# A two-layer decoder trunk on one core: tile addresses, the last down projection by token rows, and the first loads rearranged

## The chip, the core and the metric

The kernel runs on one core of one Trainium2 chip. The core has TensorE (matrix products, in the profile PE, with its weight loads as PEld), VectorE (DVE), ScalarE (ACT), GpSimd (POOL) and SyncE (SP, which here only issues DMAs). Operands lie in SBUF, 128 partitions wide; products are accumulated in PSUM, in 8 banks of 512 float32 columns. The metric is the device time of one execution in microseconds (us), as the median of several runs. One execution was also profiled.

## The reference

For one sequence of 256 tokens and width 1024, two layers of

```python
x = x + 0.5 * swiglu(rmsnorm(x, ffn1_norm[l]), ffn1_w_gate[l], ffn1_w_up[l], ffn1_w_down[l])
h = rmsnorm(x, mix_norm[l])
proj = h @ w_in[l]          # q, k/v, gates, GLA q/k/v, low rank, r, merge gates
o_a = nsa_attention(...)    # compressed, selected and window branches, 8 heads
o_b = gla_attention(...)    # gated linear attention, 4 heads, times silu(r)
y = gm[:, :, 0] * (o_a @ w_branch_nsa[l]) + gm[:, :, 1] * (o_b @ w_branch_gla[l])
x = x + y @ w_out[l]
x = x + 0.5 * swiglu(rmsnorm(x, ffn2_norm[l]), ffn2_w_gate[l], ffn2_w_up[l], ffn2_w_down[l])
```

and then `rmsnorm(x, final_norm)`. All is float32. `swiglu` is `(silu(x @ w_gate) * (x @ w_up)) @ w_down` with an inner width of 2816.

## The kernel before, in words

**Layout.** x is kept transposed: eight tiles of 128 features x 256 tokens. A product in float32 precision is made of three products of fp32r parts: an operand is split into a high part (a cast) and a low part (the rest). `mm3` (L122 to L124) issues high x high, high x low and low x high. `mm2` (L129, L130) does the same with two: the stationary weights' high part against a moving tile that holds high and low side by side (512 columns), then the weights' low part against the moving high part (256 columns). Each matmul loads its stationary tile of 128 columns again.

**Weights.** The class `Weights` streams 224 chunks of up to 128 x 2048 floats from HBM in the order of use. SP loads a chunk into one of three `raw` buffers, ACT casts the high part wh (L76), DVE subtracts to get the low part wl (L86), each in two halves; `prep` casts one half and subtracts the half before, and the program calls it twice a chunk, so that about one and a half chunks are ready ahead. Three pairs of wh and wl buffers take turns.

**Stages of a layer.** `ffn` (gate and up: 22 chunks of 16 rows, mm2 with x as the moving tile, profile name ff), down (16 chunks of 11 rows, name dn: eight output blocks of 22 products, mm2 for seven of them, mm3 for the last, with the hidden tiles h as moving tiles), `mixer` (T_pair products, name mm<-xs,wh, mm3 with 256 moving columns of x; the two vg chunks; 16 wr chunks, name mm<-wh,xs, in which a 128-token piece of x is stationary and 512 columns of weights move, mm3, in eight blocks of two chunks: v, v, r, r and four blocks of the merge gate gm; the merge, 6 wb chunks, name mg, the same form with oa and ob stationary; the output projection wo, 4 chunks, mm2 with y moving for seven of eight blocks), and `ffn` again. Attention and GLA run as generators whose steps are put between the mixer's matmuls (`slot`).

**Norms.** A norm's sum of squares goes through TensorE (`stat`, name st), then DVE (ms, L192) and a power on POOL (`rstd_col`, L194); `rstd_row` (name rb) turns it into a row with a product against the identity. The first chunk or two of a stage run before the norm is known; their results wait in PSUM (`wait`) and are scaled later.

**PSUM.** Two pools: `mm` with two banks and `sd` with six. The mixer's blocks take both banks of `mm`; a block of r leaves its banks by ACT (tanh) and then DVE (L541, which writes rt).

**Start.** ACT issues four loads of x and one of sm (all norm weights and biases); SP issues four loads of the first weight chunk, then the second chunk in three pieces and the third. Seven warm-up products (wb) run before the data come. Then x and chunk 0 are split in four steps, chunk 1 is cast, x is squared (L1153), the squares are summed on DVE (L1182 to L1185), and chunk 1's second half and chunk 2 are prepared.

**End.** In the last down projection the finished x blocks are multiplied by the final norm's weights and transposed back by TensorE (fin). After the last block come square, column sums (stl), power, four scalings, and four output DMAs on SP's queue.

**Addresses.** SBUF pools lie one behind the other in the order in which `go` opens them, each slot rounded to 32 bytes: const, small, sq, rb, t4 (15 tiles of 4096 bytes a partition, among them h, y, oa and ob), t2, raw, w. In the program before, the tiles of xs start at 128 modulo 512 bytes, and those of t4, t2, raw and of both w tags at 480 modulo 512. Weight rows of 128 columns, of 512 columns, and the high and low halves of a tile, lie at multiples of 512 bytes within their tiles.

## Time and profile before

| | |
|---|---|
| median of three runs | 1268.01 us (1267.92 to 1268.65) |
| profiled execution, whole | 1268.17 us |
| its span, first to last instruction | 1266.4 us |
| mean granted TensorE clock | 0.998 of full speed |
| busy share: PE, PEld, DVE, ACT, POOL | 99%, 85%, 72%, 56%, 4% |
| moved by DMA | 227.43 MB, 180 GB/s on average |

A row of a timeline gives the start, the length and the engine of an instruction, its source line, what it writes and reads, and in brackets how long its engine had been idle and what it waited for. The lengths of matmuls are modelled and overlap: what a matmul costs in a stream is the distance to the next start.

### The profile page before, as it was taken

The numbers are of one execution on the slowest core, as the hardware profiler recorded it, in microseconds if no ns is written. First come the engines' busy times: TensorE is split into PE (matmuls) and PEld (weight loads), VectorE is DVE, ScalarE is ACT, GpSimd is POOL, SyncE is SP. The second block draws the span as 40 slices with busy tenths as digits, with TensorE's granted clock in tenths as the row PEclk, the third lists the DMA queues.
The fourth block names the chain that finished last, engine by engine and source line by source line (L and its number), as shares of the span: only waits on it lengthen the run. The fifth ranks groups of instructions, "written<-read, shape, count | busy, mean of one in ns | idle before, by whom it ended". The sixth has DMA issues, their size and how long they took to land.

```text
span 1266.4 us, 18985 instructions
## 1 busy us (share of the span) xinstructions
PE 1251.6 (99%) x7396; PEld 1076.0 (85%) x7396; DVE 913.9 (72%) x1690; ACT 711.8 (56%) x1265; POOL 50.5 (4%) x60
## 2 busy tenths in 40 slices
PE   9999999999999999999999999999999999999997
PEld 7888889987778888888888888999777788888886
DVE  6888766774755778886578886567656668888753
ACT  5666545566644556655456664456675445566542
POOL 2001101000010000000010000010000100000000
PEclk9999999999999999999999999999999999999999
DMA  7576767334534445545665546573344354555451
GB/s 272 193 230 211 255 201 264 132 124 137 178 118 144 181 168 205 187 154 198 209 224 208 179 150 205 173 283 135 111 156 164 103 199 148 184 200 185 165 190 59
DMA packets 41001, 227.43 MB, mean 180 GB/s; under 512 B 6949, under 2 KB 8109, under 8 KB 21328
## 3 DMA queue, kind: packets, MB, share of 16 engines
q1 hardware_dynamic: 34352, 213.27, 48.7%
q0 software_dynamic: 5840, 11.87, 2.8%
q8 instruction: 58, 0.95, 0.3%
q10 hardware_dynamic: 720, 1.09, 0.3%
q14 instruction: 31, 0.25, 0.1%
HBM read 225.12 MB, written 2.63 MB: 180 GB/s over the span
## 4 chain that ended last, share of the span: by engine, by line
PE 80%; issue 15%; DVE 2%; ACT 2%; DMA 1%; POOL 0%; POOLq 0%; DVEq 0%; ACTq 0%
PE ff L129 19%; PE ff L130 10%; PE dn L129 9%; PE mm L122 7%; PE mm L123 6%; PE mm L124 6%; PE dn L130 4%; PE wo L129 2%; PE mg L122 2%; PE mg L124 2%; PE mg L123 2%; PE O L150 2%; PE o L150 1%; PE s L150 1%; PE wo L130 1%
## 5 line engine op out<-in xcount | busy, mean ns | idle before, releaser
L76 ACT ACTIVATE wh<-raw 128x1024 fp32r<-128x1024 f32 (+3 forms) x445 | 423.4, 967 | 183.6 <-issue 112.3
L86 DVE TENSOR_TENSOR wl<-raw,wh 128x1024 fp32r<-128x1024 f32 (+3 forms) x445 | 491.3, 1119 | 44.0 <-ACT wh L76 43.7
L129 PE MATMUL ff<-xs,wh 128*128 128x512 f32 x1408 | 489.9, 392 | 0.4 <-DVE xs L162 0.4
L130 PE MATMUL ff<-xs,wl 128*128 128x256 f32 x1408 | 393.9, 280 | 0.7 <-DVE wl L1144 0.5
L129 PEld LDWEIGHTS ff<-xs,wh 128*128 128x128 f32 x1408 | 264.4, 188 | 59.2 <-ACT wh L1143 0.8
L130 PEld LDWEIGHTS ff<-xs,wl 128*128 128x128 f32 x1408 | 264.3, 188 | 1.7 <-DVE wl L1144 1.1
L129 PE MATMUL dn<-h,wh 128*128 128x512 f32 x616 | 218.3, 399 | 0.0
L130 PE MATMUL dn<-h,wl 128*128 128x256 f32 x616 | 173.0, 281 | 0.0
L129 PEld LDWEIGHTS dn<-h,wh 128*128 128x128 f32 x616 | 115.7, 188 | 28.3
L139 DVE TENSOR_TENSOR u<-ff,u 128x256 f32<-128x256 f32 x176 | 74.7, 425 | 60.9 <-ACT u L138 60.9
L130 PEld LDWEIGHTS dn<-h,wl 128*128 128x128 f32 x616 | 116.4, 189 | 0.0
L122 PE MATMUL mm<-wh,xs 128*128 128x512 f32 x256 | 106.2, 415 | 2.5 <-DVE rt L541 2.5
L123 PE MATMUL mm<-wl,xs 128*128 128x512 f32 x256 | 101.5, 396 | 0.0
L124 PE MATMUL mm<-wh,xs 128*128 128x512 f32 x256 | 100.9, 394 | 0.0
L249 ACT ACTIVATE u<-u 128x256 f32<-128x256 f32 x88 | 36.8, 419 | 90.8 <-DVE u L248 90.8
L261 ACT ACTIVATE h<-u 128x256 fp32r<-128x256 f32 x88 | 36.8, 418 | 83.9 <-DVE u L260 83.9
L122 PE MATMUL mm<-xs,wh 128*128 128x256 f32 x256 | 73.8, 288 | 0.0
L124 PE MATMUL mm<-xs,wl 128*128 128x256 f32 x256 | 71.7, 280 | 0.0
L123 PE MATMUL mm<-xs,wh 128*128 128x256 f32 x256 | 71.6, 280 | 0.0
L138 ACT ACTIVATE u<-ff 128x256 f32<-128x256 f32 x176 | 65.6, 373 | 9.8 <-PE ff L130 5.4
L355 DVE SCALAR_TENSOR_TENSOR xs<-dn,xs 128x256 f32<-128x256 f32 x60 | 25.5, 424 | 56.0 <-PE dn L130 38.5
L122 PEld LDWEIGHTS mm<-wh,xs 128*128 128x128 f32 x256 | 48.1, 188 | 19.3 <-issue 4.7
(244 smaller groups left out, 1618.1 us busy)
## 6 DMA issues: line engine op xcount, KB each, us to landing
raw<-in_gu SPq DMA_DIRECT2D x85, 1024.0 KB, 4.9
raw<-in_wd SPq DMA_DIRECT2D x64, 704.0 KB, 4.1
raw<-in_wr SPq DMA_DIRECT2D x32, 1024.0 KB, 4.8
raw<-in_wt SPq DMA_DIRECT2D x16, 1024.0 KB, 5.1
raw<-in_wb SPq DMA_DIRECT2D x12, 1024.0 KB, 4.8
w<-in_w POOLq DMA_DIRECT2D x16, 512.0 KB, 8.6
raw<-in_wo SPq DMA_DIRECT2D x8, 1024.0 KB, 4.9
raw<-in_vg SPq DMA_DIRECT2D x4, 592.0 KB, 3.7
```

The source lines that it names most:

```text
L76: self.nc.scalar.activation(wh[:, s], self.raw[c][:, s], AF.Copy)
L86: self.nc.vector.tensor_sub(wl[:, s], self.raw[c][:, s], wh[:, s].bitcast(F32))
L122: mm(out, lh, rh, start=first, stop=False, skip_group_check=True)
L123: mm(out, lh, rl, start=False, stop=False, skip_group_check=True)
L124: mm(out, ll, rh, start=False, stop=last, skip_group_check=True)
L129: mm(b, lh, x[2], start=first, stop=False, skip_group_check=True)
L130: mm(b[:, 0:T], ll, x[0], start=False, stop=last, skip_group_check=True)
L138: self.nc.scalar.activation(o, b[:, T : 2 * T], AF.Copy)
L139: self.nc.vector.tensor_add(o, b[:, 0:T], o)
L150: self.nc.tensor.matmul(out, l, r, start=first, stop=last, skip_group_check=True)
L249: nc.scalar.activation(g, g, AF.Silu)
L261: nc.scalar.activation(hs[i][0], h, AF.Copy)
```

## The change

- The w tiles are 2176 instead of 2048 floats wide, and chunks whose weights move in 512 (or 296) columns (vg, wr, wb and the new wl) are written 40 floats further on. A tile of 128 floats that nothing uses is put ahead of t4, one of 88 floats ahead of w; the scratch of software DMAs is halved to 8192 bytes.
- The last down projection is computed with token rows in the partitions: 11 chunks of 4 rows of 512 columns, mm3 with h stationary; x comes in by products with the identity; squares, weights and scaling follow for each half of the features and of the tokens. The factor 0.5 goes into the gate of that stage. The final norm's weights come as a broadcast row from POOL's queue in chunk 11 of the gate and up stage.
- x's second to fourth loads are issued by SP, sm is the first load of ACT.
- The first norm's statistics come after chunk 1 instead of halfway through it, and its use in chunk 2; the first chunks' subtraction of wl comes ahead of the squares.
- The second block of r takes banks of `sd`.

```diff
+SHIFT = 40
...
-                self.pools["w"].tile([P, 2048], F32R, name=f"w{x}{c}", tag=f"w{x}") for x in "hl"
+                self.pools["w"].tile([P, 2176], F32R, name=f"w{x}{c}", tag=f"w{x}") for x in "hl"
...
-        self.nc.scalar.activation(wh[:, s], self.raw[c][:, s], AF.Copy)
+        self.nc.scalar.activation(wh[:, s.start + off : s.stop + off], self.raw[c][:, s], AF.Copy)
...
         def gate2(u):
-            nc.vector.tensor_mul(u[:, 0:T], u[:, 0:T], self.rbc)
+
+            if next_gain is None:
+                nc.vector.scalar_tensor_tensor(u[:, 0:T], u[:, 0:T], 0.5, self.rbc, op0=OP.mult, op1=OP.mult)
+            else:
+                nc.vector.tensor_mul(u[:, 0:T], u[:, 0:T], self.rbc)
...
+            late = i < 2 and start
+            if i == 1 + start:
+                self.rstd_row("mm" if start else "sd")
+                for n, b in enumerate(wait):
+                    u = gate(n, b[0])
+                    if start and n == 0:
+                        W.prep()
+                    gate2(u)
+                    up(n, u, b[1])
+            if not late:
                 u = gate(i, bs[0])
             W.prep()
...
+            if late:
+                self.stat("mm")
+                self.rstd_col()
+                self.constants()
+                wait.append(bs)
             else:
                 up(i, u, bs[1])
-                W.prep()
-            low()
+            W.prep()
+            if late:
+                continue
+            while len(lows) > 1:
+                low()
...
+        if next_gain is None:
+            self.last_down(hs)
+            return
...
+    def last_down(self, hs):
+
+        nc, W = self.nc, self.W
+        bs = [[self.bank(f"dn{e}{tt}", "sd" if e else "mm") for tt in range(2)] for e in range(2)]
+        pre = [self.small([P, 2], f"pre{tt}", 1) for tt in range(2)]
+        xg = [[self.t2(f"xg{e}{tt}") for tt in range(2)] for e in range(2)]
+
+        def residual(e):
+            for tt in range(2):
+                for q in range(4):
+                    self.mm(bs[e][tt][:, q * P : q * P + P], self.x[4 * e + q][:, tt * P : tt * P + P], self.ident, q == 0, False)
+
+        def products(c, tt, wh, wl):
+            for r in range(4):
+                e, k = divmod(4 * c + r, NFF)
+                s = slice(tt * P, tt * P + P)
+                self.mm3(bs[e][tt], hs[k][0][:, s], hs[k][1][:, s], wh[:, r], wl[:, r], False, k == NFF - 1)
+
+        def gained(e, tt):
+            sq = self.t2(f"fsq{e}{tt}")
+            nc.scalar.activation(sq, bs[e][tt], AF.Square, accum_out=pre[tt][:, e : e + 1])
+            nc.vector.tensor_mul(xg[e][tt], bs[e][tt], self.fin[:, e * 512 : e * 512 + 512])
+
+        def first(tt):
+            gained(0, tt)
+            nc.vector.tensor_scalar(pre[tt][:, 0:1], pre[tt][:, 0:1], 1.0 / D, EPS, op0=OP.mult, op1=OP.add)
+
+        def finish(tt):
+            gained(1, tt)
+            ms = self.small([P, 1], "fms")
+            nc.vector.tensor_scalar(ms, pre[tt][:, 1:2], 1.0 / D, pre[tt][:, 0:1], op0=OP.mult, op1=OP.add)
+            rs = self.small([P, 1], "frs")
+            nc.gpsimd.tensor_tensor(rs, ms, self.mhalf[:, 0:1], op=OP.pow)
+            for e in range(2):
+                o = xg[e][tt]
+                if e == 0:
+                    nc.scalar.activation(o, o, AF.Copy, scale=rs)
+                    nc.scalar.dma_start(self.out[tt, :, 0:512], o)
+                else:
+                    nc.vector.tensor_scalar(o, o, rs, None, op0=OP.mult)
+                    nc.sync.dma_start(self.out[tt, :, 512:1024], o)
+
+        residual(0)
+        for c in range(8):
+            if c == 5:
+                residual(1)
+            wh, wl = W.take()
+            for tt in range(2):
+                products(c, tt, wh, wl)
+                W.prep()
+            if c in (3, 4):
+                W.prep()
+            if c == 5:
+                for tt in range(2):
+                    first(tt)
+        ws = [W.take() for _ in range(3)]
+        for tt in range(2):
+            for x in range(3):
+                products(8 + x, tt, *ws[x])
+            finish(tt)
...
-            block(r_evac(n))
+            block(r_evac(n), ("mm", "sd")[n])
...
+            gap = pool("gap", 1)
+            gap.tile([P, 128], F32, name="gap0")
             self.pt4 = pool("t4", 15)
             self.pt2 = pool("t2", 9)
-            pools = dict(raw=pool("raw", N_RAW), w=pool("w", N_SPLIT))
+            pools = dict(raw=pool("raw", N_RAW))
+            pool("gap2", 1).tile([P, 88], F32, name="gap1")
+            pools["w"] = pool("w", N_SPLIT)
...
+                wide = lambda n, k, c: [(a[n][l, i], 4, c, SHIFT) for i in range(k)]
...
-            sm = cp.tile([P, 80], F32, name="sm")
+            sm = cp.tile([P, 72], F32, name="sm")
...
-            for p in range(4):
-                nc.scalar.dma_start(self.xs[:, 2 * p : 2 * p + 2, :], a["x"][:, 2 * p : 2 * p + 2, :])
-                nc.sync.dma_start(view(first, p), view(a["gu"][0, 0, 0], p))
-                if p == 0:
-                    nc.scalar.dma_start(sm, a["sm"])
...
+            nc.scalar.dma_start(sm, a["sm"])
+            nc.scalar.dma_start(self.xs[:, 0:2, :], a["x"][:, 0:2, :])
+            for p in range(4):
+                if p:
+                    nc.sync.dma_start(self.xs[:, 2 * p : 2 * p + 2, :], a["x"][:, 2 * p : 2 * p + 2, :])
+                nc.sync.dma_start(view(first, p), view(a["gu"][0, 0, 0], p))
...
-            for n in range(7):
+            for n in range(6):
...
             for p in range(4):
-                for j in (2 * p, 2 * p + 1):
-                    self.split_x(j, gain(0, 0)[:, j : j + 1])
+                self.split_x(2 * p, gain(0, 0)[:, 2 * p : 2 * p + 1])
                 nc.scalar.activation(view(w0[0], p), view(first, p), AF.Copy)
                 nc.vector.tensor_sub(view(w0[1], p), view(first, p), view(w0[0], p).bitcast(F32))
+                self.split_x(2 * p + 1, gain(0, 0)[:, 2 * p + 1 : 2 * p + 2])
...
             W.load(1 + N_RAW)
+            W.cast()
+            W.prep()
             sq = [self.t4(f"sq{x}") for x in range(2)]
...
-            W.cast()
             nc.vector.tensor_add(sq[0], sq[0], sq[1])
...
-            W.prep()
...
+                def gain_row(i):
+                    if i == 11:
+                        self.fin = self.t4("fin")
+                        nc.gpsimd.dma_start(self.fin, a["fin"].broadcast_to([P, D]))
...
-    nc = _bacc.Bacc("TRN2", target_bir_lowering=False, num_devices=1)
+    nc = _bacc.Bacc("TRN2", target_bir_lowering=False, num_devices=1, dynamic_dma_scratch_size=8192)
```

## Rows read from the trace of the kernel before

**Rows 1.** The page's first part: busy us (share of the span), instructions.
```profile
PE 1251.6 (99%) x7396; PEld 1076.0 (85%) x7396; DVE 913.9 (72%) x1690; ACT 711.8 (56%) x1265; POOL 50.5 (4%) x60
```
**Rows 2.** Timeline of PE in gate and up of the second stage: start, length.
```profile
480.05 0.39 PE L129 MATMUL ff<-xs,wh 128*128 128x512 f32 x1
...
485.94 0.39 PE L129 MATMUL ff<-xs,wh 128*128 128x512 f32 x1
```
**Rows 3.** Timeline of PE, down of the same stage.
```profile
571.22 0.40 PE L129 MATMUL dn<-h,wh 128*128 128x512 f32 x1
...
625.63 0.28 PE L122 MATMUL dn<-h,wh 128*128 128x256 f32 x1
```
**Rows 4.** Timeline of PE in the wr block and the merge of layer 0.
```profile
383.23 0.39 PE L122 MATMUL mm<-wh,xs 128*128 128x512 f32 x1
...
387.43 0.39 PE L122 MATMUL mm<-wh,xs 128*128 128x512 f32 x1
...
393.40 0.39 PE L122 MATMUL mg<-wh,oa 128*128 128x512 f32 x1
...
399.52 0.39 PE L122 MATMUL mg<-wh,ob 128*128 128x512 f32 x1
```
**Rows 5.** Waits of PE over the span: us in total, times, longest us.
```profile
PE mm L122 <- DVE rt L541: 2.5, 2, 1.2
```
**Rows 6.** Timeline of the last down projection and the end.
```profile
1193.51 0.40 PE L129 MATMUL dn<-h,wh 128*128 128x512 f32 x1
...
1257.41 0.28 PE L124 MATMUL dn<-h,wl 128*128 128x256 f32 x1
...
1259.60 0.69 POOL L194 TENSOR_TENSOR rs<-ms,mhalf 128x2 f32<-128x2 f32 x1 [181.08 <-DVE ms L192]
...
1260.32 1.41 DVE L1231 TENSOR_SCALAR out<-fin,rs 128x512 f32<-128x512 f32 x2 [0.80 <-POOL rs L194]
1261.04 1.80 SPq L1232 DMA_DIRECT2D out<-out  x4
```
**Rows 7.** Timeline of the start.
```profile
10.88 0.91 ACT L161 ACTIVATE xs<-xs,sm 128x256 fp32r<-128x256 f32 x2 [0.66 <-DMA xs<-in_x]
...
13.09 0.38 PE L130 MATMUL ff<-xs,wl 128*128 128x256 f32 x1 [0.23 <-DVE wl L1144]
13.26 1.99 ACT L1153 ACTIVATE sq<-xs 128x1024 f32<-128x1024 f32 x2
15.28 1.23 DVE L1182 TENSOR_TENSOR sq<-sq,sq 128x1024 f32<-128x1024 f32 x1 [1.05 <-ACT sq L1153]
...
17.75 0.61 PE L150 MATMUL st<-ones,acc 128*128 128x1 f32 x4 [0.46 <-DVE acc L1185]
...
20.11 1.60 POOL L194 TENSOR_TENSOR rs<-ms,mhalf 128x2 f32<-128x2 f32 x1 [19.66 <-DVE ms L192]
...
21.77 0.71 PE L150 MATMUL rb<-cst,rs 128*128 128x128 f32 x4
22.24 0.48 PE L129 MATMUL ff<-xs,wh 128*128 128x512 f32 x1
...
27.88 0.39 PE L129 MATMUL ff<-xs,wh 128*128 128x512 f32 x1
```
**Rows 8.** Timeline behind the second r block of layer 1.
```profile
949.46 0.49 PE L122 MATMUL mm<-wh,xs 128*128 128x512 f32 x1 [1.23 <-DVE rt L541]
...
950.61 1.22 DVE L86 TENSOR_TENSOR wl<-raw,wh 128x1024 fp32r<-128x1024 f32 x1
```
**Rows 9.** Groups of ACT by shape: busy us, mean ns, idle before.
```profile
L849 ACT ACTIVATION_READ_ACCUMULATOR on<-o 128x1 f32 x16 | 3.2, 199 | 0.0
```
**Rows 10.** Stretches of the start: length, ACT busy, PEclk, DMA share, GB/s.
```profile
0.00:8.00 8.00, 3.26 (x7) 1.00 0.69 219
8.00:12.00 4.00, 3.34 (x8) 1.00 1.00 352
12.00:15.00 3.00, 3.00 (x5) 1.00 1.01 391
```

More of the change, by code (lines that the diff above doesn't have):

```diff
@@ L49, in load @@
         while self.n_load < min(n, len(self.chunks)):
-            ap, rows, cols = self.chunks[self.n_load]
+            ap, rows, cols, _ = self.chunks[self.n_load]
             t = self.pools["raw"].tile([P, 2048], F32, name=f"raw{self.n_load}", tag="raw")
@@ L85, in prep @@
         wh, wl = self.split[c]
-        self.nc.vector.tensor_sub(wl[:, s], self.raw[c][:, s], wh[:, s].bitcast(F32))
+        off = self.chunks[c][3]
+        o = slice(s.start + off, s.stop + off)
+        self.nc.vector.tensor_sub(wl[:, o], self.raw[c][:, s], wh[:, o].bitcast(F32))
         self.n_prep = (c, part)
@@ L96, in take @@
             self.prep()
-        _, rows, cols = self.chunks[c]
+        _, rows, cols, off = self.chunks[c]
         wh, wl = self.split.pop(c)
-        return tuple(x[:, : rows * cols].rearrange("p (r c) -> p r c", c=cols) for x in (wh, wl))
+        return tuple(x[:, off : off + rows * cols].rearrange("p (r c) -> p r c", c=cols) for x in (wh, wl))
 class Trunk:
@@ L164, in split_x, with square @@
         )
-    def square(self, j, own=False):
+    def square(self, j):
         sq = self.psq.tile([P, T], F32, name=f"sq{self.uid()}", tag="sq" if j else "acc")
@@ L226, in lead_pair @@
             self.rstd_col()
-    def final_x(self, j):
-        if j == 0:
-            self.fin = [[self.bank(f"fin{t}{e}") for e in range(2)] for t in range(2)]
-        xg = self.xg.pop(j)
-        for tt in range(2):
-            self.nc.tensor.transpose(self.fin[tt][j // 4][:, j % 4 * P : j % 4 * P + P], xg[:, tt * P : tt * P + P], self.ident)
     def ffn(self, l, f, next_gain, hook=None):
@@ L280, in ffn @@
                 W.prep()
-                wait = bs
+                wait = [bs]
                 continue
@@ L284, in ffn @@
                 self.mm2(bs[0], wh[:, k], wl[:, k], self.xx[k], k == 0, k == NK - 1)
-            if i == 1:
-                if start:
-                    self.stat()
-                    self.rstd_col()
-                    self.constants()
-                else:
-                    self.rstd_row()
-                    u0 = gate(0, wait[0])
-                    gate2(u0)
-                    up(0, u0, wait[1])
-            if not (i == 1 and start):
+            late = i < 2 and start
[8 more added lines that the diff above has]
+            if not late:
                 u = gate(i, bs[0])
             W.prep()
-            if not (i == 1 and start):
+            if not late:
                 gate2(u)
@@ L329, in ffn @@
                     W.prep()
-                if next_gain is None and half == 0 and j > 0:
-                    self.final_x(j - 1)
-                    if j == NK - 1:
-                        self.st = self.bank("stl")
-                        self.sums(self.acc, True, False)
-            self.add_half(j, b)
-            if next_gain is None:
-                self.square(j, own=j == NK - 1)
-                xg = self.t2(f"xg{j}")[:, 0:T]
-                nc.vector.tensor_scalar(xg, self.x[j], self.final[:, j : j + 1], None, op0=OP.mult)
-                self.xg[j] = xg
-            else:
-                self.post_x(j, next_gain[:, j : j + 1])
+            self.add_half(j, b)
+            self.post_x(j, next_gain[:, j : j + 1])
         W.prep()
@@ L509, in mixer, with block @@
                 T_pair(lambda ps: scaled(t3[:, 2 * i : 2 * i + 2], ps, c))
-        def block(evac):
-            bs = [self.bank(f"mm{self.uid()}", "mm") for _ in range(2)]
+        def block(evac, tag="mm"):
+            bs = [self.bank(f"mm{self.uid()}", tag) for _ in range(2)]
             for half in range(2):
@@ L1218, in go @@
                 self.mixer(l, gain(l, 2))
-                self.ffn(l, 1, gain(l + 1, 0) if l + 1 < L else None)
-            self.sums(self.own, False, True)
-            self.rstd_col()
-            self.final_x(NK - 1)
-            for tt in range(2):
-                for e in range(2):
-                    o = self.t2(f"out{tt}{e}")
-                    b = self.fin[tt][e]
-                    if e == 0:
-                        nc.scalar.activation(o, b, AF.Copy, scale=self.rs[:, tt : tt + 1])
-                    else:
-                        nc.vector.tensor_scalar(o, b, self.rs[:, tt : tt + 1], None, op0=OP.mult)
-                    nc.sync.dma_start(self.out[tt, :, e * 512 : e * 512 + 512], o)
+                self.ffn(l, 1, gain(l + 1, 0) if l + 1 < L else None, gain_row if l + 1 == L else None)
 def _bucket(n):
```

62 lines of the change are left out of this document (28 added, 34 removed).

## The prediction

> **What bounds the kernel now.** Read the engine shares first: TensorE's matmuls are busy for 99% of the span [rows 1]. Its queue is the time; other engines count only where it waits for them. Since matmuls are pipelined, look next at the distance between starts, in the timeline. Four stretches without a wait give four pitches, and they differ where the columns do not:
>
> - gate and up (mm2: a moving operand of 512 columns, then one of 256): 17 pairs from 480.05 to 485.94, 346.5 ns a pair [rows 2];
> - down, the same mm2: 154 pairs (7 output blocks of 22) from 571.22 to the first mm3 at 625.63, 353.3 ns a pair [rows 3];
> - the wr block (mm3, 512 columns each): 18 matmuls from 383.23 to 387.43, 233.3 ns each [rows 4];
> - the merge, the same mm3: 27 matmuls from 393.40 to 399.52, 226.7 ns each [rows 4].
>
> Set these beside the addresses that the section on the kernel gives. Call the distance the address of the stationary tile minus that of the moving one, modulo 512 bytes. Gate and up: weights 480, xs 128, distance 352. Down: weights 480, h 480, distance 0. wr: xs 128, moving weights 480, distance 160. Merge: ob 480, moving weights 480, distance 0. So mm2 is cheaper at 352 than at 0, and mm3 with 512 columns cheaper at 0 than at 160; output projection wo (y in t4) is an mm2 at 0. Last come the waits inside the queue: the mixer's wait for rt [rows 5], the end [rows 6] and the start [rows 7].
>
> A rule of the Trainium skill speaks against this reading: "TensorE: Matmul & The Clock Gate", section "Step-by-step: what each phase is for", says that TensorE has two independent read ports on SBUF, so that loading the next weights takes nothing from the running matmul. By it the pitch would hang on columns alone; two mm3 streams of 512 columns at 233.3 and 226.7 ns [rows 4] do not agree. What it would make of the time is the first rival's.
>
> **The change, part by part.** The sum stands against the profiled execution, 1268.17 us (span 1266.4); the median of the runs is 0.16 lower.
>
> *Addresses.* sm shrinks by 32 bytes; pre0, pre1, fms and frs are six new slots of 32 bytes; the gap adds 512; the smaller scratch moves all by 8192. So t4 goes from 480 to 480-32+192+512 = 1152, which is 128 modulo 512; t2 and raw follow; the second gap (352 bytes) puts w back at 480, and a slot of 8704 bytes keeps it there. A shift of 40 elements is 160 bytes: shifted weights stand at 640, so 128. Then gate and up stay at 352; down and wo move from 0 to 352; wr from 160 to 0; the merge stays at 0. Priced by the row of the same form at the new distance:
> - wr: 768 matmuls (2 layers, 16 chunks, 24 each) by 6.7 ns is 5.1 us. Many stand right behind a small matmul of the side work, where the pitch has not settled; I take 4.5. Bounds 0 and 5.1.
> - down: three of the four stages keep mm2, 3 x 154 pairs by 6.8 ns = 3.2 us; wo, 2 x 56 pairs, 0.8. Together 4.0; bounds 0 and, if a pair could cost 1.5 x 226.7 = 340.0, 7.6. The short mm3 of the last block and vg count nothing.
> - gate and up: 0. Only wl moves against wh, by a multiple of 512. Weight rows are 512 bytes apart, so a chunk's 16 rows pass through all such multiples already, and rows 2 are their mean. No row shows the new pairing; its far ends are 353.3 and 340.0 ns, 9.6 us worse or 9.2 better over 1408 pairs, and I stay at 346.5.
>
> *The second r block on the other PSUM pool.* The first merge-gate block waits for rt to leave the bank of the block before: 1.2 us, twice in all, 2.5 [rows 5]. With r's second block elsewhere it takes banks left long before. Next late would be its second weight chunk: the split that runs at 950.61 for 1.22 us ends at 951.83; the block, which started at 949.46 [rows 8], would start 1.2 earlier and need that chunk 24 matmuls on, about 953.7. Gain 2.5; bounds 0 and, counted from start to start (949.46 against 233 ns after the last of r), some 2.8.
>
> *Last down projection in token rows.* Before: 63.90 us from its first matmul at 1193.51 to the last start at 1257.41 [rows 6]. After: 22 x 2 x 2 x 3 = 264 matmuls of mm3 at distance 0, 59.8 us at 226.7 ns, plus 16 full-precision products of x with the identity. Nearest is rb, 128 columns, in the same precision: four records for two products, from 21.77 to the next start at 22.24 [rows 7], so 3.8 for all. Sum 63.6: gain 0.3. Bounds -1.5 (233.3 ns) and 0.9. Weights arrive in chunks of 24 matmuls (5.4 us); two to three halves split in each cost VectorE 1.22 us apiece, so they hide. fin (512 KB on POOL's queue) is issued ten chunks ahead of its first use and hides in gate and up.
>
> *The end.* Before, from the last matmul's start: residual, square, column sums, power (1259.60, 0.69), two scalings on each engine (1.41), four output issues on one queue from 1261.04 for 1.80: last issue done 5.43 us after 1257.41 [rows 6]. After: 0.4 to leave PSUM (the 0.28 of the last matmul's row and 0.11 for 256 more columns), a square as long as a scaling of that shape, 0.7, its accumulator read 0.20 [rows 9], ms and the hand-overs 0.35 (an estimate), power 0.69, one scaling 0.70, one issue 0.45 on each of two queues: 3.5. The first token half went out eight us earlier. Gain 1.9; with a power of 1.60, as in the start [rows 7], 1.0; upper bound 2.2, as two transfers land instead of four.
>
> *The start.* SP issues seven DMAs in a row (at the end's 0.45 apiece, some 3.2 us, ahead of chunk 1's), ACT only sm and the first x; ACT's table load is no longer behind its queue. But bytes decide: x, sm and chunk 0 are 2.14 MB, and 1.75 had come at 8.0 (219 GB/s) with 352 GB/s after it [rows 10], so the last is moved at 9.1 and lands about 9.6, and not at 10.88 [rows 7]. A cast and a subtraction later, 1.5 us, the last quarter of chunk 0 starts near 11.1; before it reached wl at 13.09. Then comes what is moved: cast and split of chunk 1 and the first cast of chunk 2 stand ahead of the squares on ACT. Chunk 2's first half completes 3.8 MB, at 13.6 by 391 GB/s [rows 10], landed 14.1; its cast, as long as a square of that shape (1.0), ends at 15.1, the squares (1.99) at 17.1, and the sums (15.28 to the statistics at 17.75: 2.4) at 19.5. TensorE ends chunk 1 at 18.1 and waits 1.4 there; queued behind are chunk 2's gate (its wl split follows the sums: 20.7), then rb behind the power. Chunk 2 ends about 27.1 instead of 27.88 [rows 7]: gain 0.8. Bounds -0.5 (VectorE has three gates to finish and is late with chunk 4) and 2.0 (nothing of the lead lost). The norm weights land first and cost nothing; POOL's constants leave about 2 us later, ahead of chunk 5.
>
> *The rest at nothing.* gate2 of the last stage is one VectorE instruction of the same shape as before, `low` a chunk later only moves VectorE's work within a chunk, and a warm-up product fewer ends while the first quarter is still being split; its cover gone, it would cost at most what is left of the start's 0.8.
>
> Sum: 4.5 + 4.0 + 2.5 + 0.3 + 1.9 + 0.8 = 14.0. 1268.17 - 14.0 = 1254.2, as a median 1254.0.
>
> **The rivals.**
> 1. *Pitch belongs to the stage, not to the distance.* No tile is seen at two distances in this trace, and stages differ in other ways (where the moving tile lies, whose turn 256 columns are). Then addresses give nothing and the last down runs at 233.3 ns, 1.5 behind: 2.5 + 1.9 + 0.8 - 1.5 = 3.7 gained, 1264.3. The skill's rule above comes to this. Against it: four pitches sort by distance. Chance 0.12.
> 2. *A wait takes the place of rt.* VectorE runs without a break there, and the next split may be late: 2.5 less, 1256.5. Against: some 1.8 us of margin (953.7 against 951.8). 0.08.
> 3. *The gap tiles take no room, since nothing writes them.* The change then does not do what it says: without the 352 bytes w starts at 128, and gate and up fall from distance 352 to 0, 1408 pairs by 6.8 ns = 9.6 us; down and wo gain nothing, wr at an unseen distance is put at nothing, last down 1.5 behind, 5.2 gained at the two ends and at rt. 9.6 + 1.5 - 5.2 is 5.9 slower: 1273.9. It decides from 2.6 ns a pair. For it: no instruction names a gap tile. Against: a pool reserves what is asked of it. 0.04.
>
> **How the numbers follow.** Forecast 0.71, rivals 0.12, 0.08 and 0.04; 0.05 for a better layout effect (the bound of 340 ns). The forecast's own range is 1250 to 1258 from the bounds above; reaching toward the first rival, 1249.5 to 1260.5 leaves some 0.2 out. Within 0.2% (2.5 us, about what a measurement of this kernel can tell from no change) only a half-failed first rival or a mild third falls: 0.03. Slower is the third rival and what would go wrong unseen: 0.05. Faster: 0.92.
>
> **What would show it.** Right: down pairs at 346 to 347 ns; wr in triples of 0.68 us; gate and up still at 346.5; no wait for rt; 3.5 us from the last matmul to the last issue; the fourth gate chunk (27.88 now) starting near 27. The prediction is wrong if down stays at 353 or wr at 233 (first rival), if gate and up rise to 353 (third), if the first merge-gate block waits for wl (second), or if statistics in the start wait past 20.

## The result, and the profile after

1256.61 us, median of 4 (1256.44 to 1256.85), against 1267.97 (1267.55 to 1268.65): ratio 0.991, 95% interval 0.9893 to 0.9927. The forecast was 1254.0, the range 1249.5 to 1260.5. The profiled execution took 1256.44 us, its span is 1254.7, 11.7 less than before. Lines move: mm3 is now L129 to L131, mm2 L136 and L137, the cast L81, the split's subtraction L93.

Two rows of the page: TensorE is again busy 99% of the span, as in [rows 1], with 104 matmul records fewer.

```profile
span 1254.7 us, 18722 instructions
...
PE 1241.6 (99%) x7292; PEld 1071.0 (85%) x7292; DVE 903.1 (72%) x1658; ACT 710.2 (57%) x1255; POOL 50.8 (4%) x62
```

The timeline of down in the second stage, which answers to [rows 3], and of wr in layer 0, which answers to [rows 4] (start, length, then the matmul):

```profile
567.93 0.39 PE L136 MATMUL dn<-h,wh 128*128 128x512 f32 x1
...
621.31 0.28 PE L129 MATMUL dn<-h,wh 128*128 128x256 f32 x1
```

```profile
382.54 0.39 PE L129 MATMUL mm<-wh,xs 128*128 128x512 f32 x1
...
383.21 0.39 PE L129 MATMUL mm<-wh,xs 128*128 128x512 f32 x1
...
383.89 0.39 PE L129 MATMUL mm<-wh,xs 128*128 128x512 f32 x1
...
384.57 0.39 PE L129 MATMUL mm<-wh,xs 128*128 128x512 f32 x1
```

154 pairs of down in 53.38 us are 346.6 ns each (353.3 before), and wr runs in triples of 0.67 to 0.68 (0.70 before). TensorE's waits over the span (us in total, times, longest) no longer hold the wait for rt of [rows 5]. The two longest are now these, of which the first was 0.4 before and the second not there:

```profile
PE ff L136 <- DVE xs L169: 1.9, 1, 1.9
PE ff L137 <- DVE wl L93: 1.4, 1, 1.4
```

Both are in the start, which answers to [rows 7]. First its stretches (length; busy us and count of PE, PEld, DVE, ACT, POOL; granted clock as a share of 2.4 GHz; DMA share; GB/s), then its timeline:

```profile
6.00:8.00 2.00, 0.26 (x1) 0.19 (x1) 0.85 (x2) 1.43 (x4) 0.00 (x0) 1.00 1.08 400
8.00:10.00 2.00, 1.83 (x6) 1.43 (x6) 2.00 (x5) 2.00 (x5) 0.00 (x0) 0.58 1.07 345
10.00:12.00 2.00, 2.00 (x9) 1.71 (x8) 2.00 (x6) 2.00 (x6) 0.00 (x0) 0.57 1.02 390
12.00:14.00 2.00, 2.00 (x14) 1.75 (x13) 2.00 (x4) 1.66 (x3) 0.00 (x0) 1.00 1.05 415
```

```profile
7.74 0.47 PE L136 MATMUL ff<-xs,wh 128*128 128x512 f32 x1 [1.86 <-DVE xs L169]
...
14.79 1.06 ACT L81 ACTIVATE wh<-raw 128x1024 fp32r<-128x1024 f32 x1 [0.39 <-DMA raw<-in_gu]
...
15.76 1.99 ACT L1213 ACTIVATE sq<-xs 128x1024 f32<-128x1024 f32 x2
...
20.89 0.50 PE L157 MATMUL st<-ones,acc 128*128 128x1 f32 x4
...
22.62 1.61 POOL L199 TENSOR_TENSOR rs<-ms,mhalf 128x2 f32<-128x2 f32 x1 [22.17 <-DVE ms L197]
...
24.28 0.71 PE L157 MATMUL rb<-cst,rs 128*128 128x128 f32 x4
...
27.61 0.39 PE L136 MATMUL ff<-xs,wh 128*128 128x512 f32 x1
...
33.16 0.40 PE L136 MATMUL ff<-xs,wh 128*128 128x512 f32 x1
...
33.73 1.22 DVE L93 TENSOR_TENSOR wl<-raw,wh 128x1024 fp32r<-128x1024 f32 x1
...
35.01 0.39 PE L137 MATMUL ff<-xs,wl 128*128 128x256 f32 x1 [1.45 <-DVE wl L93]
```

TensorE has used up its warm-up products near 5.9, idles 1.86 us, and then runs most of its first pairs at half rate (granted clock 0.58 and 0.57, which is 1.2 GHz for part of each stretch and 2.4 for the rest). At 33.16 it starts the fifth gate chunk (chunk 4 of the prediction, which counts from 0) and must wait until 35.01 for a low half that VectorE splits only at 33.73.

The end, answering to [rows 6]:

```profile
1184.23 1.95 PE L157 MATMUL dn<-cst,xs 128*128 128x128 f32 x16
...
1247.48 0.39 PE L131 MATMUL dn<-wh,h 128*128 128x512 f32 x1
1247.90 0.60 ACT L367 ACTIVATE fsq<-dn 128x512 f32<-128x512 f32 x1 [5.21 <-PE dn L131]
...
1249.52 0.55 POOL L379 TENSOR_TENSOR frs<-fms,mhalf 128x1 f32<-128x1 f32 x1 [7.58 <-DVE fms L377]
1250.10 0.72 ACT L383 ACTIVATE xg<-xg,frs 128x512 f32<-128x512 f32 x1 [1.51 <-POOL frs L379]
...
1250.85 0.35 ACTq L384 DMA_DIRECT2D out<-xg  x1
```

By stages, from the first matmul of each in both timelines (differences taken from the traces' nanoseconds, then rounded). The start ends with the first down matmul, before and after:

```profile
134.20 0.40 PE L129 MATMUL dn<-h,wh 128*128 128x512 f32 x1
```

```profile
135.67 0.39 PE L136 MATMUL dn<-h,wh 128*128 128x512 f32 x1
```

| term | forecast gain | measured gain |
|---|---|---|
| wr and the second r block, two layers | 4.5 + 2.5 | 6.57 (122.22 to 118.94, 122.23 to 118.94) |
| T pairs and vg, two layers | 0 | -0.26 (71.23 to 71.36, 71.23 to 71.35) |
| down (three stages) and wo | 4.0 | 4.33 (62.32 to 61.13 each; 24.32 to 23.94) |
| last down, first to last matmul start | 0.3 | 0.66 (63.91 to 63.25) |
| end, from there to the end of the span | 1.9 | 1.80 (8.98 to 7.19) |
| start, to the first down matmul | 0.8 | -1.47 (134.20 to 135.67) |
| gate and up, merge | 0 | 0.10 |
| sum | 14.0 | 11.73 |

All terms but one are near their forecast. The start has the wrong sign, and its 2.27 us are most of the 2.6 by which 1256.61 misses 1254.0. That 1256.61 is what the second rival forecast (1256.5) is a coincidence: no matmul of the mixer waits for wl, and wr with the second r block gained 6.57 of 7.0.

### The profile page after: what moved, and what is told of

Same layout as the page of the kernel before. It is cut to its first block, busy times and chain, and to the rows that moved or that the text cites. A ratio compares the mean times of both kernels' runs of the same rounds, so it can differ in the third digit from the quotient of the medians.

```text
span 1254.7 us, 18722 instructions
## 1 busy us (share of the span) xinstructions
PE 1241.6 (99%) x7292; PEld 1071.0 (85%) x7292; DVE 903.1 (72%) x1658; ACT 710.2 (57%) x1255; POOL 50.8 (4%) x62
## 4 chain that ended last, share of the span: by engine, by line
PE 96%; DVE 1%; issue 1%; ACT 1%; DMA 0%; POOLq 0%; POOL 0%; ACTq 0%
PE ff L136 25%; PE ff L137 13%; PE dn L136 8%; PE mm L129 7%; PE mm L131 7%; PE mm L130 7%; PE dn L137 4%; PE dn L131 2%; PE dn L129 2%; PE dn L130 2%; PE wo L136 2%; PE mg L129 2%; PE mg L131 2%; PE mg L130 2%; PE O L157 2%; PE o L157 1%
## 5 line engine op out<-in xcount | busy, mean ns | idle before, releaser
L93 DVE TENSOR_TENSOR wl<-raw,wh 128x1024 fp32r<-128x1024 f32 (+3 forms) x435 | 489.8, 1141 | 58.9 <-ACT wh L81 58.6
L81 ACT ACTIVATE wh<-raw 128x1024 fp32r<-128x1024 f32 (+3 forms) x435 | 421.6, 985 | 175.4 <-issue 83.1
L136 PE MATMUL ff<-xs,wh 128*128 128x512 f32 x1408 | 491.0, 393 | 1.9 <-DVE xs L169 1.9
L137 PE MATMUL ff<-xs,wl 128*128 128x256 f32 x1408 | 394.5, 280 | 1.6 <-DVE wl L93 1.4
L136 PEld LDWEIGHTS ff<-xs,wh 128*128 128x128 f32 x1408 | 265.1, 188 | 60.9 <-ACT wh L1200 2.2
L137 PEld LDWEIGHTS ff<-xs,wl 128*128 128x128 f32 x1408 | 265.1, 188 | 2.2 <-DVE wl L93 1.8
L136 PE MATMUL dn<-h,wh 128*128 128x512 f32 x462 | 160.3, 392 | 0.0
L137 PE MATMUL dn<-h,wl 128*128 128x256 f32 x462 | 129.1, 280 | 0.0
L129 PE MATMUL mm<-wh,xs 128*128 128x512 f32 x256 | 104.9, 410 | 0.0
L136 PEld LDWEIGHTS dn<-h,wh 128*128 128x128 f32 x462 | 86.7, 188 | 19.2
L131 PE MATMUL mm<-wh,xs 128*128 128x512 f32 x256 | 100.2, 391 | 0.0
L137 PEld LDWEIGHTS dn<-h,wl 128*128 128x128 f32 x462 | 86.7, 188 | 0.0
L129 PE MATMUL mm<-xs,wh 128*128 128x256 f32 x256 | 73.8, 288 | 0.0
L131 PE MATMUL mm<-xs,wl 128*128 128x256 f32 x256 | 71.8, 280 | 0.0
L129 PEld LDWEIGHTS mm<-wh,xs 128*128 128x128 f32 x256 | 48.1, 188 | 14.3 <-issue 4.7
L131 PEld LDWEIGHTS mm<-wh,xs 128*128 128x128 f32 x256 | 48.1, 188 | 10.7
```

The costliest lines, as they stand in the source:

```text
L81: self.nc.scalar.activation(wh[:, s.start + off : s.stop + off], self.raw[c][:, s], AF.Copy)
L93: self.nc.vector.tensor_sub(wl[:, o], self.raw[c][:, s], wh[:, o].bitcast(F32))
L129: mm(out, lh, rh, start=first, stop=False, skip_group_check=True)
L131: mm(out, ll, rh, start=False, stop=last, skip_group_check=True)
L136: mm(b, lh, x[2], start=first, stop=False, skip_group_check=True)
L137: mm(b[:, 0:T], ll, x[0], start=False, stop=last, skip_group_check=True)
```

## Experiments

Two questions: does the distance of the two operands set the pitch, or the stage; and what went wrong in the start. All ratios below are to the kernel before.

**Every chunk at another distance.** In two gate and up stages, two down stages and both wr stages each weight chunk stands at its own offset.

```
+            step = lambda l, i, on: (8 * (i % 16) + 4 * l) if on else 0
-                        chunks.append((a["gu"][l, f, i], 16, P, 0))
+                        chunks.append((a["gu"][l, f, i], 16, P, step(l, i, f + l == 1)))
...
-                wide = lambda n, k, c: [(a[n][l, i], 4, c, SHIFT) for i in range(k)]
+                wide = lambda n, k, c: [(a[n][l, i], 4, c, step(l, i, True) if n == "wr" else SHIFT) for i in range(k)]
```

> The changed kernel with the weights of two gate and up stages, two down stages and both wr stages standing at another distance in every chunk, in steps of 32 bytes in one layer and 16 bytes between them in the other; the rest as it is. One look, to read the pitch of each chunk. Theory A (the pitch is set by the distance of stationary and moving tile modulo 512 bytes): the pitch differs from chunk to chunk and is the same for gate and up and for down at the same distance: 346.5 ns a pair at 352, 353 at 0, and for three-product matmuls of 512 columns 226.7 at 0 and 233.3 at 160; the other distances lie between 340 and 356 and between 224 and 236 ns. Rival D (pitch belongs to the stage, first rival of the prediction): every chunk of a stage has the same pitch, 346.5 in gate and up, within 1 ns.

1262.25 us in its one run. Four chunk starts of one gate and up stage, 16 pairs from one row to the next of a couple; the first couple is at distance 256, the second at 352:

```profile
519.78 0.40 PE L136 MATMUL ff<-xs,wh 128*128 128x512 f32 x1
...
525.43 0.40 PE L136 MATMUL ff<-xs,wh 128*128 128x512 f32 x1
...
536.72 0.40 PE L136 MATMUL ff<-xs,wh 128*128 128x512 f32 x1
...
542.28 0.40 PE L136 MATMUL ff<-xs,wh 128*128 128x512 f32 x1
```

5.65 us against 5.56 for the same work in the same stage. The mean pitch by distance, worked out from the starts in this trace (ns; a pair of mm2 in gate and up and in down, a matmul of wr; values at d and d + 256 agree within 0.5 ns in gate and up wherever both occur, except for 160 to 192, where they differ by up to 2.2; for wr without the pitches over 250 ns, behind side work; the 353.7 of down at 160 is 350.3 without two pitches of 388). For all three rows d is the stationary tile's address minus the moving one's:

```
d mod 256    0    16    32    48    64    80    96   112   128   144   160   176   192   208   224   240
gate, up 353.2 346.7 353.1 346.9 352.6 352.9 346.7 352.9 350.9 349.2 351.1 350.5 351.8 349.5 347.4 347.0
down     352.6 346.7 352.4 346.9 352.3 352.3 346.7 353.5 351.3 349.4 353.7 349.6 352.9 349.1 346.7 346.8
wr       229.6 234.7 232.6 232.7 233.4 232.3 233.4 232.8 233.0 231.7 233.5 231.3 229.7 233.0 232.9 231.5
```

Gate and up and down agree at nearly every distance, and one stage runs at 347 or 353 as its chunk stands. The first rival (pitch belongs to the stage) is refuted. In the scan only the weights move and the moving tiles stay at 128, so by itself it could also be read as a rule on the weights' own address. The down stages speak against that: weights at 480 take 353.3 ns with h at 480 and 346.6 with h at 128, and weights and moving tile both at 128 (distance 0 of the scan) take 353 again.

Three details were not expected: the pattern repeats after 256 bytes, not 512; no distance is cheaper than 346.7, so the change's 352 is already as good as any; and for wr 0 and 192 are lowest, 2 to 5 ns below the rest, not 6.7. Two limits remain. At distances 432 and 448 two chunks of one stage differ at the same distance (353.2 and 349.3 ns, 348.9 and 353.3 ns), so there distance alone does not settle the pitch, and no run shows what else does. And the chunk means of wr also hang on the place in the stage (226.7 to 232.4 in the changed kernel, where every chunk stands at 0), so differences of a few ns between single distances in its row are not shown. The Trainium skill ("TensorE: Matmul & The Clock Gate", section "Step-by-step: what each phase is for") has the weight load on a read port of its own that takes nothing from the running matmul. By that no pitch would hang on where the two operands stand; the 6 to 7 ns a pair between 96 and 0 show that it does for these operands.

**Addresses alone, on the kernel before.** Gap tiles, wider slots, the shift and the smaller scratch; every instruction as before.

```
+            pool("gap", 1).tile([P, 40], F32, name="gap0")
...
+            pool("gap2", 1).tile([P, 88], F32, name="gap1")
...
-                self.pools["w"].tile([P, 2048], F32R, name=f"w{x}{c}", tag=f"w{x}") for x in "hl"
+                self.pools["w"].tile([P, 2176], F32R, name=f"w{x}{c}", tag=f"w{x}") for x in "hl"
```

> The kernel before with the addresses alone changed: gaps ahead of t4 and w, weight slots of 8704 bytes, the shift of 160 bytes, the smaller scratch; all instructions as before. Theory A (distance sets the pitch): each of the four down stages 1.1 to 1.2 us shorter (pairs at 346.5 instead of 353.3), wr 2.0 to 2.5 shorter per layer, wo 0.4 per layer, gate and up unchanged: 1258.6 (1258.0 to 1259.5). Rival D (pitch belongs to the stage): 1268.0.

1260.78 us (1260.49 to 1261.13), ratio 0.9942, interval 0.9928 to 0.9956: 7.2 gained, 2.2 short of the 1258.6 expected. Down 1.19 a stage and wo 0.38 a layer as expected, gate and up unchanged; the last down (old form) gained 0.83 (63.08), and T pairs with vg lost 0.15 a layer (71.38). wr fell short, 1.14 a layer. One reason is that its mean pitch is 229.0 and not 226.7 ns; its waits give another:

```profile
PE mm L124 <- DVE rt L543: 3.2, 2, 1.6
```

TensorE comes earlier to a bank that VectorE leaves no earlier: the wait for rt grew from 1.2 to 1.6 each.

**The second r block alone, on the kernel before.**

```
-            block(r_evac(n))
+            block(r_evac(n), ("mm", "sd")[n])
```

> The kernel before with one edit: the second r block takes its two PSUM banks from the six-bank pool. The prediction's term is 2.5 us (two waits of 1.2 us), up to 2.8: 1265.4. The changed kernel against the one with the addresses alone lost 2.15 us per layer in the wr stage, so if the edit is worth that by itself it gives 4.3: 1263.7. Theory F (with faster wr the wait for rt grows, 1.2 to 1.6 us, so part of the layout's gain showed up only with this edit): the edit alone gives 2.5 to 3.4, 1264.6 to 1265.5, and the sum of the two edits made alone is 0.5 to 1.5 us short of both together.

1264.22 us (1263.97 to 1264.60), ratio 0.9972, interval 0.9961 to 0.9983: 3.6 gained. In the traces, whose spans are 4.0 apart, the wr stage is 1.73 a layer shorter, 3.45 in all; the other 0.58 is the start, which varies (see the last section). The prediction priced the wait by its row, 1.2. These are the two matmuls around it in layer 0 of the kernel before:

```profile
325.56 0.39 PE L124 MATMUL mm<-wh,xs 128*128 128x512 f32 x1
327.18 0.50 PE L122 MATMUL mm<-wh,xs 128*128 128x512 f32 x1 [1.23 <-DVE rt L541]
```

The pitch there is 1.62 where 0.23 is normal, so 1.39 is lost; the next three matmuls with a stretched pitch (0.34, 0.35 and 0.34 from 327.18, 329.86 and 330.20 on) cost 0.32 more. Alone the edits give 1.14 + 1.73 = 2.87 a layer, together 3.28: part of what the addresses give in wr reaches the end only when the wait for rt is gone. That is theory F: the sum is 0.8 short over two layers, as it has it. The edit alone is a little over F's 2.5 to 3.4, and the time lies between F's range and the 1263.7 of the other forecast.

**The whole start of before, in the changed kernel.**

```
-                if p:
-                    nc.sync.dma_start(self.xs[:, 2 * p : 2 * p + 2, :], a["x"][:, 2 * p : 2 * p + 2, :])
+                nc.scalar.dma_start(self.xs[:, 2 * p : 2 * p + 2, :], a["x"][:, 2 * p : 2 * p + 2, :])
...
-            if i == 1 + start:
-                self.rstd_row("mm" if start else "sd")
+            if i == 1:
+                if start:
+                    self.stat()
```

> The changed kernel with the whole start of the kernel before: x loads issued by the scalar engine, norm weights second, seven warm-up products, both casts of x ahead of each quarter's split, and the first norm's sums in the middle of the second gate chunk. If the start is what my sum missed, the first down matmul comes 1.5 us earlier (about 128.0 instead of 129.5 us from the first gate matmul's 7.6) and the time is 1255.1 (1254.8 to 1255.4). If the stages behind it lost that time on their own (addresses, new waits), the start gives nothing back: 1256.4 to 1256.8.

1254.50 us (1254.41 to 1254.76), ratio 0.9895, interval 0.9879 to 0.9912: 2.1 less than the changed kernel, more than forecast. (The 129.5 us of the expectation is in no trace: from the first gate matmul to the first down the changed kernel takes 127.9, this run 126.0.) So the start is where the time went.

**Only the norm of before; the loads as changed, 8 warm-up products.**

```
-            late = i < 2 and start
...
+            if i == 1:
+                if start:
+                    self.stat()
+                    self.rstd_col()
```

> The changed kernel with the first norm back where it was before (sums in the middle of the second chunk), but with the loads as changed (sync engine, norm weights first, split of x alternating) and 8 warm-up products. Theory A (the moved norm is what cost the start; the loads cost and give nothing): 1254.5 as with the whole start of before (1254.2 to 1254.8). Rival E (the loads are part of the loss, since first x now comes second on its queue): 1255.2 or more, with the first gate matmul or the later quarters of chunk 0 late by what is lost.

1254.67 us (1254.58 to 1254.79), ratio 0.9894, interval 0.9881 to 0.9908. The loads cost nothing that could be told and gave nothing: the second gate chunk starts at 14.00 here (first row) and at 14.02 with the whole start of before (second row).

```profile
14.00 0.39 PE L136 MATMUL ff<-xs,wh 128*128 128x512 f32 x1
```

```profile
14.02 0.39 PE L136 MATMUL ff<-xs,wh 128*128 128x512 f32 x1
```

The moved norm, with the order of work that came with it, lost the two microseconds.

**Two more warm-up products.**

```
-            for n in range(6):
+            for n in range(8):
```

> The changed kernel with 8 instead of 6 warm-up products, so that TensorE is not left idle from 5.89 to 7.74 us; nothing else differs. Both theories expect the granted clock at 1.00 instead of 0.58 between 8 and 12 us, so the first five pairs of gate and up at 0.35 instead of 0.64 us each. Theory A (VectorE's queue sets the start): the 1.4 us won there are given back as a wait at the column sums (their operand is ready at 20.2) and at rb (its power stands behind two splits and ends at 24.2), so rb stays at 24.1 to 24.3 us, the fifth gate chunk waits as before until 35.0, and the time stays within 0.3 us of 1256.6. Rival B (the halved clock is what the start lost): everything behind it moves up, the first down matmul is 1.4 us earlier, and the time is 1255.1 to 1255.3.

1256.61 us (1256.56 to 1256.64), ratio 0.9911, interval 0.9897 to 0.9926: no change. The clock was mended (stretches, as above), though TensorE still idles 1.56 us ahead of the first gate matmul, and the timeline shows where the 1.4 us went:

```profile
8.00:10.00 2.00, 1.83 (x9) 1.33 (x10) 2.00 (x5) 2.00 (x6) 0.00 (x0) 1.00 1.07 366
10.00:12.00 2.00, 2.00 (x13) 1.78 (x13) 2.00 (x6) 2.00 (x5) 0.00 (x0) 1.00 1.03 376
```

```profile
20.40 0.61 PE L157 MATMUL st<-ones,acc 128*128 128x1 f32 x4 [0.68 <-DVE acc L1244]
...
24.43 0.71 PE L157 MATMUL rb<-cst,rs 128*128 128x128 f32 x4
...
35.17 0.39 PE L137 MATMUL ff<-xs,wl 128*128 128x256 f32 x1 [1.46 <-DVE wl L93]
```

TensorE came 1.3 earlier to the column sums and waited there for the accumulator; rb and the wait of the fifth chunk stand where they stood, 0.15 later. The Trainium skill ("TensorE: Matmul & The Clock Gate", section "HAM oscillation — how this bites in real kernels") warns that a wait for data lets the clock fall, and that the next work then starts slow. The trace of the changed kernel agrees that far (0.58 behind an idle of 1.86 us), but by that alone the mended clock would have brought the 1.4 us, and it brought none: VectorE's queue set the end of the start.

**One split ahead in VectorE's queue.**

```
-                    if start and n == 0:
+                    if start:
                         W.prep()
...
-            W.prep()
+            if not (start and i == 2):
+                W.prep()
```

> The changed kernel with one split moved in VectorE's queue: the low half of the fifth gate chunk's first part is made behind the second gate (near 30.4 us) instead of behind the third (33.73 us). Theory A (VectorE's queue of three postponed gates sets the wait at 33.16): that wait of 1.6 us goes, no other of that size takes its place, and the time is 1255.0 (1254.8 to 1255.3). Rival C (the split is late because its weights or a slot for them are late, not because of what stands ahead of it): the split still runs near 33.7 and the time stays at 1256.6. Rival B (only the halved clock costs): 1256.6 as well, the wait moved elsewhere.

1256.70 us (1256.35 to 1258.33), ratio 0.9915, interval 0.99 to 0.9929: no change, so theory A's 1255.0 missed. In the profiled execution (1258.33; weights landed late, and rb came at 26.20) the wait for that split is gone, and the next half has one:

```profile
38.01 0.40 PE L136 MATMUL ff<-xs,wh 128*128 128x512 f32 x1
...
38.40 1.22 DVE L93 TENSOR_TENSOR wl<-raw,wh 128x1024 fp32r<-128x1024 f32 x1
...
39.67 0.38 PE L137 MATMUL ff<-xs,wl 128*128 128x256 f32 x1 [1.27 <-DVE wl L93]
```

The backlog had only been passed on, in this execution, which was the slowest of the four. The time is that of the rivals, the reason neither's: the split left its place (against C), and a mended clock alone gives nothing (against B).

**Squares ahead of the cast that waits for its DMA** (with 8 warm-up products).

```
             W.cast()
-            W.prep()
             sq = [self.t4(f"sq{x}") for x in range(2)]
...
+            W.prep()
```

> The changed kernel with 8 warm-up products and with ScalarE's two squares of x ahead of the first cast of chunk 2 instead of behind it (that cast waits for its DMA). Theory A (the order on ScalarE and VectorE sets rb): squares from 14.4 instead of 15.76, accumulator ready at 18.9 instead of 20.2, rb at 23.0 to 23.2 instead of 24.3 to 24.4, the fifth gate chunk still waits some 1.6 us for its split behind three gates, and the time is 1255.2 (1255.0 to 1255.5). Rival B (the clock and the arrival of the data set the start, the norm hides): no change against 1256.6.

1255.39 us (1255.05 to 1255.74), ratio 0.99, interval 0.9886 to 0.9913: 1.2 gained, as theory A had it. The matmul of rb is at 23.51 (24.28 in the changed kernel, 24.43 with the warm-up products alone), less early than expected because the data came late in this execution: the squares start at 14.99. The wait in the fifth chunk is whole:

```profile
23.51 0.71 PE L157 MATMUL rb<-cst,rs 128*128 128x128 f32 x4
...
34.23 0.39 PE L137 MATMUL ff<-xs,wl 128*128 128x256 f32 x1 [1.46 <-DVE wl L93]
```

**The same, with both later splits one place ahead** (the added split of the run with one split ahead; in its place the last split of the third chunk is left to the next one).

```
-                    if start and n == 0:
+                    if start:
                         W.prep()
...
-            W.prep()
+            if not (start and i == 2):
+                W.prep()
             if late:
```

> As the run with the squares ahead, and in the third gate chunk both later splits stand one place further ahead in VectorE's queue (the low half of chunk 4's first part behind the second gate, of its second part behind the third), so that neither stands behind all three gates. In the earlier run that moved only one split, the wait of 1.6 us went and one of 1.4 us came at the next half. Theory A: both waits go, 1253.7 (1253.4 to 1254.3). Rival C (three gates are more than VectorE can do between rb and chunk 5, whatever their order): a wait of over a microsecond stays near 33 to 40 us, and the time is that of the run without the move, 1255.2.

1254.83 us (1254.75 to 1255.15), ratio 0.9896, interval 0.9882 to 0.9909: between the two forecasts. The wait moved again, to the sixth chunk, and shrank to 1.18:

```profile
37.46 0.40 PE L136 MATMUL ff<-xs,wh 128*128 128x512 f32 x1
37.61 1.22 DVE L93 TENSOR_TENSOR wl<-raw,wh 128x1024 fp32r<-128x1024 f32 x1
...
38.88 0.39 PE L137 MATMUL ff<-xs,wl 128*128 128x256 f32 x1 [1.02 <-DVE wl L93]
```

**The same, with the two postponed gates finished together.** Each gate goes from VectorE to ScalarE and back; one after the other, VectorE stands idle at each hand-over.

```
+                    for n, b in enumerate(wait):
+                        us.append(gate(n, b[0]))
+                        W.prep()
+                    for u in us:
+                        gate2(u)
+                    ups([0, 1], us, [b[1] for b in wait])
```

`ups` is `up` for both: the halves of both, then the products of both.

> As the run with the squares and the splits ahead, and the two postponed gates are no longer finished one after the other but step by step together (first halves of both, second halves of both, then both products), so that VectorE does not stand idle for ScalarE between the steps (it stood idle 2.2 us in all between rb and chunk 5 in that run). Theory A (VectorE's queue of three gates, with its hand-overs to ScalarE, is what is late): the split of chunk 5's first part, at 37.61 there, comes 1.0 to 1.3 us earlier and the wait of 1.18 us at 37.46 shrinks to 0.2 or less: 1253.7 (1253.5 to 1254.1). Rival C (VectorE's work itself is too much there): the wait stays above 0.8 us, 1254.6 or more.

1253.74 us (1253.57 to 1253.83), ratio 0.9889, interval 0.9874 to 0.9904. The split of the sixth chunk comes at 36.52 instead of 37.61 (first fence), and TensorE's waits between 8 us and the first down (second fence) are down to two:

```profile
36.52 1.22 DVE L93 TENSOR_TENSOR wl<-raw,wh 128x1024 fp32r<-128x1024 f32 x1
```

```profile
PE ff L136 <- ACT wh L1218: 1.2, 1, 1.2
PE ff L137 <- DVE wl L1219: 0.2, 1, 0.2
```

Both are at the first pair of the first gate chunk. VectorE's work was not too much; what made it late was its order, with the hand-overs. This version is 0.2% under the changed kernel (their ranges don't touch) and 1.1% under the one before. Against the run with the norm of before, which has the same loads and warm-up products, it gains some 0.8 (1254.67 to 1253.74, with 1267.96 and 1267.80 for the kernels of before beside them): the moved norm is worth something once VectorE's queue behind it is put in order.

**That version with 6 warm-up products.**

```
-            for n in range(8):
+            for n in range(6):
```

> As the run with the paired gates, but with the change's 6 warm-up products instead of 8, so that TensorE idles from about 5.9 us and the granted clock is near 0.58 from 8 to 12 us again. In the changed kernel itself the 1.4 us lost there were swallowed by the later waits for the norm; here only some 0.4 us of such waits are left (column sums and rb). Theory A (a halved clock costs only what no later wait swallows): the column sums come at 20.9 instead of 19.5, rb at 24.0 to 24.2 instead of 23.05, and the time is 1254.7 (1254.5 to 1255.1). If the loss is swallowed here too: 1253.7, with rb at 23.1.

1254.33 us (1254.01 to 1254.48), ratio 0.9891, interval 0.9875 to 0.9908: 0.6 more by the medians, 0.8 in the traces, somewhat under theory A's 1.0; rb is at 23.96 (23.05 with 8), as A had it. Granted clock:

```profile
8.00:10.00 2.00, 2.00 (x6) 1.38 (x7) 2.00 (x5) 2.00 (x6) 0.00 (x0) 0.50 1.06 321
10.00:12.00 2.00, 2.00 (x10) 1.72 (x9) 2.00 (x6) 2.00 (x6) 0.00 (x0) 0.67 1.01 367
```

The same half rate that was free in the changed kernel costs here, where later waits swallow only part of it.

## Why the prediction was right, and where it was wrong

- *Reading.* TensorE's queue is the time, and its pitch hangs on the distance: right in the main, shown by the scan and by the addresses alone; it repeats after 256 bytes, not 512, and at two distances it is not the whole rule. Gate and up at no gain: right (122.94 and 122.93 us).
- *wr.* 4.5 was too much: the mean pitch without the matmuls behind side work went from 233.3 to 229.0 ns, not to 226.7; by 768 that is 3.3.
- *Second r block.* 2.5 was too little: 3.45 alone. The row of a wait tells how long the engine stood, not what the stop cost. The two errors nearly cancel (7.0 forecast, 6.57), which is luck.
- *Down and wo.* 4.0, measured 4.33; the last block's mm3, which I counted at nothing, gains too. T pairs and vg lost 0.26 that I had not counted. The loss comes with the addresses (0.30 in the run with these alone); which of the moved tiles costs it was not tried.
- *Last down.* 0.3, measured 0.66. With the addresses alone the old form takes 63.08, so token rows by themselves gave nothing in this stage; what they gave is the end.
- *The end.* 3.5 from the last matmul's start to the last issue's end, measured 3.72 (1247.48 to 1251.20).
- *The start: the step that failed.* "Chunk 2 ends about 27.1 instead of 27.88" and "gain 0.8". It ends at 27.61, 0.27 gained, though by another way: I had TensorE wait for the sums (19.5), and it came late itself, at half clock; the sums were late too (20.2), so my sign of being wrong, "statistics in the start wait past 20", came true (20.89, and 20.40 with the clock mended). The lead from the loads that I started from was not there: "TensorE ends chunk 1 at 18.1" leaves out that its 32 pairs take 11.1 us from the first gate matmul on, so from 7.74 it cannot end before 18.8 however early the data are. What came after was mis-sized: "VectorE has three gates to finish and is late with chunk 4" stood as a bound of -0.5 and not in the value. It is the largest single effect of the start: 1.74 us (1.85 from 33.16 to 35.01, where 0.23 is normal, and 0.11 in the next pitch). 0.27 - 1.74 = -1.47. It can be followed in the timeline after: rb cannot come before the power, two gates of some 2.6 us each with their hand-overs, a split and the first half of a third gate stand between rb and that split, and TensorE has 8.9 us of work from rb to the matmul that needs it. I worked out when the norm would be ready and stopped at the chunk where it is used.
- *Rivals.* The first is refuted. The second (another wait in place of rt) did not happen where I put it; a wait for a late split came in the start instead. The third is refuted: the gaps take their room, as the pitches show.

## What to carry to other kernels

When a step is moved later, follow each engine's queue to the point where it has caught up, not to the moved step: here the price stood 9 us behind it, in a split that nobody had moved. Before mending a visible loss (a halved clock, one late split), look whether a later wait already swallows it; mended alone it gives nothing, or passes the wait on. Where matmuls run back to back, one run with every weight chunk at another offset tells what the addresses are worth.

## What the runs showed of the hardware that I had not expected

- The pitch of these fp32r matmuls hangs on the distance of the two operands modulo 256 bytes, in steps finer than 32 bytes: 353.2 ns a pair at 0, 346.7 at 16, 353.1 at 32, 346.9 at 48. At 176 and 192 it also differed by 3.9 and 4.4 ns between chunks of one stage that stand at the same distance.
- The granted clock fell to half after TensorE idled 1.86 us at the start, but not after it waited 1.45 us in the fifth chunk, where the next pairs ran at 0.35 us. The length of the idle time alone does not decide it: at the start it fell behind 1.49 us (the scan), but not behind 1.56 (two more warm-up products). In the profiled execution with one split ahead it fell to 0.50 (24 to 26 us) behind waits that left TensorE busy 0.90 us of the two from 20 to 22. What decides it is not settled by these runs.
- Starts differ from one execution to the next by some 0.7 us through the arrival of data alone: before's wait that ends at 13.09 [rows 7] is missing in the run with the second r block alone, whose start has the same code (126.61 and 125.88 us from the first gate matmul to the first down). Before waited 0.66 us for the last x, which it used at 10.88; that run used it at 10.31. So part of the lead that the prediction gave to the loads was this one execution's.
